# Tree-masked attention: SyncE load of fp32 queries, warmed TensorE, leading transposes and a split last pair

## The chip, the cores and the metric

The kernel runs on one core of one Trainium2 chip. The metric is the device time of one execution in microseconds (us). A kernel's profile is that of one execution; its span is about 1.8 us shorter than the device time of the same execution.

## The reference, cut to what matters

```python
batch, heads, seq, dim = 8, 12, 512, 64          # Q, K, V: float32 (8, 12, 512, 64)
# mask[i, j] = 1 where j is i or an ancestor of i in a binary heap, else 0
scores = einsum('bhqd,bhkd->bhqk', Q, K) / sqrt(dim) + (1 - mask) * (-1e9)
weights = softmax(scores, axis=-1)
out = einsum('bhqk,bhkd->bhqd', weights, V)      # float32
```

Each of the three inputs and the output has 12.58 MB. The work is done in 48 pairs of heads, six for each batch.

## The kernel before

Cuts are marked with `# ...`.

```python
ptile = consts.tile([P, perm_np.shape[1]], bf16)        # permutations, identity first
nc.sync.dma_start(out=ptile[:, :], in_=perm_dram.ap())
ctile = consts.tile([P, code_np.shape[1]], bf16)        # mask codes, 128 x 1152
nc.vector.memset(ctile[:, :], 0.0)
for p in (0, 64):
    nc.sync.dma_start(out=ctile[p:p + 32, :], in_=code_dram.ap())
# ...
plan = [(0, Q, 0, 0, 4), (0, K, 0, 0, 4), (0, V, 0, 0, 6),
        (0, Q, 0, 4, 8), (0, K, 0, 4, 8), (0, V, 0, 6, H),
        (0, Q, 0, 8, H), (0, K, 0, 8, H), (0, Q, 1, 0, 4), # ...
# load(): GpSimd's queue, cast from fp32 to bf16 on the way
nc.gpsimd.dma_start(out=loaded[kind, b][:, h0:h1, :],
                    in_=src[b, h0:h1].rearrange("h (p t) d -> p h (t d)", t=T))
# ...
# values(i): one PSUM tile for all pairs, scaled and written in one go
o2 = psumO.tile([P, 2, 512], fp32)                      # psumO has one buffer
# ... 32 matmuls ...
nc.vector.reciprocal(out=rec, in_=o4[:, :, :, D:D + 1])
nc.vector.tensor_tensor(out=of4, in0=o4[:, :, :, 0:D], in1=rec, op=ALU.mult)
# ...
load(0, 14); transposes(0); scores(0)                   # ...
for i in range(N):
    # ... loads and GpSimd stores ...
    if i >= 4 and i + 2 < N: transposes(i + 2)
    if i + 1 < N:            scores(i + 1)
    values(i)
    if i >= N - 2:           store(nc.sync, i, 1)
    if i < 4:                transposes(i + 2)
```

The softmax here doesn't subtract the row's maximum and nothing guards it: scores larger than these inputs give would overflow.

## Time and profile before

| | kernel before |
|---|---|
| median time before the prediction | 137.62 us (3 runs) |
| span of the profiled execution | 136.5 us |
| DMA busy from 5.5 to 131 us, weighed by packets | 0.95 to 1.05 in nearly every microsecond |
| ScalarE, TensorE busy | 79%, 80% |
| last store issued | 131.60 us |
| last DMA packet ends | 135.3 us |

The profiled execution took 138.32 us, 0.7 us more than the median of the timed ones. A second profile of the same kernel, taken later (run c_before), has a span of 136.3 us; spans of its other executions lie between 135.4 and 137.3 us. So a difference of a few tenths between two single profiles says nothing, and below it is the medians and the packet counts that carry the argument.

**How the work of the DMA engines is counted.** The packet records give the size, start and duration of each packet, but not the engine. Each packet is weighed by an estimate of the engine time that it needs when nothing hinders it, from the rates and the short packets of the traces (41.6 ns for a 512-byte load packet, 42.5 for 1024 bytes, 163 for a 4096-byte store, 95 for a 2304-byte packet of codes, 660 for 16 KB of instructions, about four times a 4096-byte packet; the shortest one in the traces took 884), and the sum is divided by sixteen. "Work by 9 us" is this sum for packets that start between 0 and 9 us, in us per engine. It measures how much of the job is done, where a busy share only says that something is in flight. The whole job is 129.7 us.

### The profile page before, as it was taken

How to read it: one execution, taken by the hardware profiler on the slowest of the kernel's cores; microseconds unless marked ns; L12 is line 12 of the kernel's file. 1: busy time of each engine (PE TensorE's matmuls, PEld its weight loads, DVE VectorE, ACT ScalarE, POOL GpSimd, SP SyncE). 2: the span in 40 equal slices, each digit the busy share in tenths (PEclk: the TensorE clock that was granted, in tenths of full speed). 3: DMA queues.
4: the chain of work that ended last, by engine and by line, in shares of the span. 5: the costliest groups of instructions: out<-in, count | busy, mean ns of one | idle time of the engine just before them, and what ended most of it. 6: DMA issues, size and time to landing. Idle time of an engine off the chain costs nothing.

```text
span 136.5 us, 5468 instructions
## 1 busy us (share of the span) xinstructions
PE 109.5 (80%) x2400; PEld 80.0 (59%) x2400; DVE 98.7 (72%) x214; ACT 108.2 (79%) x145; POOL 90.4 (66%) x119
## 2 busy tenths in 40 slices
PE   0078886999986699998998998999699979989610
PEld 0035664667664467786776776777376747757400
DVE  4019678798999997889887878879677869844420
ACT  3027878799986969998998999899599979998600
POOL 6969976985696993429854497475944799932200
PEclk9999999999999999999999999999999999999995
DMA  3999999999999999999999999999999999999991
GB/s 77 165 189 197 197 197 196 197 198 198 196 199 198 198 198 199 198 244 236 195 302 253 270 207 201 338 225 272 196 248 305 246 290 240 389 377 389 394 354 41
DMA packets 41815, 32.11 MB, mean 235 GB/s; under 512 B 1280, under 2 KB 38784, under 8 KB 41792
## 3 DMA queue, kind: packets, MB, share of 16 engines
q0 software_dynamic: 41008, 30.94, 125.4%
q1 hardware_dynamic: 784, 0.84, 2.1%
q8 instruction: 18, 0.29, 0.8%
q14 instruction: 5, 0.04, 0.1%
HBM read 38.06 MB, written 12.58 MB: 371 GB/s over the span
## 4 chain that ended last, share of the span: by engine, by line
PE 41%; DVE 27%; DMA 19%; issue 5%; POOL 4%; POOLq 0%
PE o L393 16%; DVE vx L281 12%; PE st L341 10%; DVE of L407 9%; DMA qs<-in_Q_dram 7%; PE stx L341 7%; DMA out_dram<-of 7%; PE tqs L295 5%; DMA vs<-in_V_dram 5%; DVE qt L315 4%; PE tk L295 4%; DVE rec L402 3%; POOL out_dram L414 3%; POOL qs L235 1%; POOL ks L235 1%
## 5 line engine op out<-in xcount | busy, mean ns | idle before, releaser
L354 ACT ACTIVATE et<-st 128x1024 bf16<-128x1024 f32 x48 | 49.4, 1029 | 4.0 <-PE st L341 3.6
L316 ACT COPY kt<-tk 128x512 bf16<-128x512 bf16 x48 | 28.3, 590 | 15.3 <-PE tk L295 14.9
L365 ACT ACTIVATE etx<-stx 128x768 bf16<-128x768 f32 x48 | 38.9, 810 | 0.3 <-PE stx L341 0.3
L281 DVE COPY vx<-vs 32x1536 bf16<-32x1536 bf16 (+3 forms) x60 | 36.2, 603 | 3.8 <-DMA vs<-in_V_dram 2.2
L407 DVE TENSOR_TENSOR of<-o,rec 128x512 f32<-128x512 f32 x48 | 33.2, 692 | 1.7
L281 POOL COPY v<-vs 32x768 bf16<-32x768 bf16 (+1 forms) x40 | 30.2, 756 | 2.7 <-DMA vs<-in_V_dram 1.0
L295 PE MATMUL tqs<-ptile,qs 128*64 128x128 bf16 x384 | 20.1, 224 | 11.1 <-DMA qs<-in_Q_dram 6.7
L393 PE MATMUL o<-vx,etx 128*64 128x65 bf16 (+1 forms) x576 | 26.7, 198 | 2.6 <-DVE vx L281 1.5
L341 PEld LDWEIGHTS <-kt 64*128 64x128 bf16 x480 | 20.3, 95 | 11.3 <-ACT kt L316 3.6
L414 POOL DMA_DIRECT2D out_dram<-of x23 | 18.0, 784 | 11.1 <-DVE of L407 3.2
L402 DVE RECIPROCAL rec<-o 128x8 f32<-128x8 f32 x48 | 9.9, 207 | 20.6 <-PE o L393 19.3
L235 POOL DMA_DIRECT2D qs<-in_Q_dram x21 | 16.9, 806 | 11.4 <-PE o L393 4.3
L315 DVE COPY qt<-tqs 128x512 bf16<-128x512 bf16 x48 | 20.1, 418 | 6.0 <-PE tqs L295 5.1
L295 PEld LDWEIGHTS <-qs 128*64 128x64 bf16 x384 | 15.4, 111 | 12.9 <-DMA qs<-in_Q_dram 6.7
L235 POOL DMA_DIRECT2D ks<-in_K_dram x21 | 16.6, 788 | 9.7 <-DMA ks<-in_K_dram 4.2
L393 PEld LDWEIGHTS <-etx 128*64 128x64 bf16 (+1 forms) x576 | 19.5, 105 | 5.8 <-issue 3.2
L295 PE MATMUL tk<-ptile,ks 128*64 128x128 bf16 x384 | 20.4, 223 | 2.9 <-issue 2.1
L393 PE MATMUL o<-v,et 128*128 128x65 bf16 x384 | 20.3, 194 | 1.2 <-DVE of L407 1.1
L341 PE MATMUL st<-qt,kt 64*128 64x512 bf16 x96 | 18.7, 385 | 2.3 <-DVE qt L315 2.1
L341 PE MATMUL st<-ctile 64*128 64x512 bf16 x96 | 19.2, 396 | 0.1
L341 PEld LDWEIGHTS <-ctile 64*128 64x128 bf16 x192 | 11.0, 94 | 13.1 <-issue 3.0
L341 PE MATMUL stx<-qt,kt 64*128 64x128 bf16 (+1 forms) x384 | 17.9, 211 | 0.2 <-issue 0.2
(13 smaller groups left out, 58.2 us busy)
## 6 DMA issues: line engine op xcount, KB each, us to landing
out_dram<-of POOLq DMA_DIRECT2D x23, 512.0 KB, 10.7
vs<-in_V_dram POOLq DMA_DIRECT2D x6, 768.0 KB, 15.4
qs<-in_Q_dram POOLq DMA_DIRECT2D x9, 384.0 KB, 15.4
ks<-in_K_dram POOLq DMA_DIRECT2D x9, 384.0 KB, 15.3
qs<-in_Q_dram POOLq DMA_DIRECT2D x9, 256.0 KB, 11.1
ks<-in_K_dram POOLq DMA_DIRECT2D x9, 256.0 KB, 11.7
vs<-in_V_dram POOLq DMA_DIRECT2D x4, 384.0 KB, 10.1
out_dram<-of SPq DMA_DIRECT2D x2, 256.0 KB, 5.0
```

The source lines that it names most:

```text
L235: nc.gpsimd.dma_start(out=loaded[kind, b][:, h0:h1, :], in_=src[b, h0:h1].rearrange("h (p t) d -> p h (t d)", t=T),)
L281: (eng or nc.vector.tensor_copy)(out=o, in_=i)
L295: nc.tensor.matmul(out=o[D * hi:D * hi + D], rhs=perms[mat], lhsT=src[:, 2 * hp + hi, D * t:D * t + D], start=True, stop=True, is_transpos ...
L315: nc.vector.tensor_copy(out=qt[:, :], in_=tq)
L316: nc.scalar.copy(out=kt[:, :].rearrange("d (i j x) -> d i j x", j=2, x=32), in_=tk[:, :].rearrange("d (j i x) -> d i j x", j=2, x=32)[:, 0:8],
L341: nc.tensor.matmul(out=dst, lhsT=lhsT, rhs=rhs, start=first, stop=True, skip_group_check=not first,)
L354: nc.scalar.activation(out=et1[:, :, :], in_=st1[:, :, :], func=AF.Exp, scale=scale)
L365: nc.scalar.activation(out=etx[:, :, :, 32:P], in_=stx[:, :, :].rearrange("p h (t q) -> p h t q", t=T)[:, :, :, 32:P], func=AF.Exp, scale= ...
L393: nc.tensor.matmul(out=o2[p0:p1, hi, (D + 1) * t:(D + 1) * (t + 1)], lhsT=e[:, hi, P * t + p0:P * t + p1], rhs=v, start=hi not in (m[0] fo ...
L402: nc.vector.reciprocal(out=rec[:, :, :, :], in_=o4[:, :, :, D:D + 1])
L407: nc.vector.tensor_tensor(out=of4, in0=o4[:, :, :, 0:D], in1=rec[:, :, :, :].to_broadcast([P, 2, T, D]), op=ALU.mult,)
L414: eng.dma_start(out=out[b, 2 * hp:2 * hp + 2 * n].rearrange("h (p t) d -> p h (t d)", t=T), in_=done[i // 2][:, 2 * (i % 2):2 * (i % 2) + ...
```

## The change

Its intent: four heads of Q come as fp32 by SyncE's queue, which can start before GpSimd's, and are cast by GpSimd in SBUF; nine identity matmuls bring TensorE to full clock while it waits; transposes go ahead of the scores from pair 1 on, not from pair 4; the last pair's values go to a scores bank that is free, and each of its heads is scaled and stored by itself.

```diff
+    first = consts.tile([P, 4, T * D], fp32)
+    nc.sync.dma_start(
+        out=first[:, :, :], in_=Q[0, 8:12].rearrange("h (p t) d -> p h (t d)", t=T)
+    )
     ptile = consts.tile([P, perm_np.shape[1]], bf16)
@@
-            (0, Q, 0, 8, H), (0, K, 0, 8, H), (0, Q, 1, 0, 4), (0, K, 1, 0, 4),
+            (0, K, 0, 8, H), (0, Q, 1, 0, 4), (0, K, 1, 0, 4),
@@ values(i); last = i == N - 1
+        if last:
+            o2 = psumS.tile([P, 2, 512], fp32, name="st1")
+        else:
+            o2 = psumO.tile([P, 2, 512], fp32)
@@ ... scaled per head where last, and then
+            if last:
+                store((nc.sync, nc.scalar)[h0], i, h0, h1)
@@ at the start
+        for n in range(9):
+            nc.tensor.matmul(out=warm[:, n % 2, :], lhsT=perms[0],
+                             rhs=ptile[:, 0:512], start=True, stop=True)
-        load(0, 14)
+        load(0, 10)
+        nc.gpsimd.tensor_copy(out=loaded["q", 0][:, 8:12, :], in_=first[:, :, :])
+        load(0, 13)
@@ in the loop
-            if i >= 4 and i + 2 < N:
+            if i == 0:
+                scores(1)
+            if i + 2 < N:
                 transposes(i + 2)
-            if i + 1 < N:
+            if 0 < i < N - 1:
                 scores(i + 1)
             values(i)
-            if i < 4:
-                transposes(i + 2)
```

More of the change, by code (lines that the diff above doesn't have):

```diff
@@ L180 @@
     AHEAD = 12
-    FIRST = (16, 18, 20, 22, 24)
+    FIRST = (15, 17, 19, 21, 23)
     LATE = 10
@@ L379, in values @@
         )
-        o2 = psumO.tile([P, 2, 512], fp32)
+        last = i == N - 1
+        if last:
+            o2 = psumS.tile([P, 2, 512], fp32, name="st1")
+        else:
+            o2 = psumO.tile([P, 2, 512], fp32)
         full, part = [], []
@@ L391, in values @@
         mms = full + part
+        if last:
+            mms.sort(key=lambda m: m[0])
         for n, (hi, p0, p1, t, e, v) in enumerate(mms):
@@ L399, in values @@
             )
-        o4 = o2[:, :, 0:T * (D + 1)].rearrange("p h (t x) -> p h t x", t=T)
-        rec = work.tile([P, 2, T, 1], fp32)
-        nc.vector.reciprocal(out=rec[:, :, :, :], in_=o4[:, :, :, D:D + 1])
         if i % 2 == 0:
@@ L405, in values, with store @@
         of = done[i // 2][:, 2 * (i % 2):2 * (i % 2) + 2, :]
+        o4 = o2[:, :, 0:T * (D + 1)].rearrange("p h (t x) -> p h t x", t=T)
         of4 = of.rearrange("p h (t d) -> p h t d", t=T)
-        nc.vector.tensor_tensor(
-            out=of4, in0=o4[:, :, :, 0:D],
-            in1=rec[:, :, :, :].to_broadcast([P, 2, T, D]), op=ALU.mult,
-        )
-    def store(eng, i, n):
+        rec = work.tile([P, 2, T, 1], fp32)
+        for h0, h1 in ((0, 1), (1, 2)) if last else ((0, 2),):
+            nc.vector.reciprocal(
+                out=rec[:, h0:h1, :, :], in_=o4[:, h0:h1, :, D:D + 1]
+            )
+            nc.vector.tensor_tensor(
+                out=of4[:, h0:h1, :, :], in0=o4[:, h0:h1, :, 0:D],
+                in1=rec[:, h0:h1, :, :].to_broadcast([P, h1 - h0, T, D]),
+                op=ALU.mult,
+            )
+            if last:
+                store((nc.sync, nc.scalar)[h0], i, h0, h1)
+    def store(eng, i, h0, h1):
         b, hp = pairs[i]
         eng.dma_start(
-            out=out[b, 2 * hp:2 * hp + 2 * n].rearrange(
+            out=out[b, 2 * hp + h0:2 * hp + h1].rearrange(
                 "h (p t) d -> p h (t d)", t=T
             ),
-            in_=done[i // 2][:, 2 * (i % 2):2 * (i % 2) + 2 * n, :],
+            in_=done[i // 2][:, 2 * (i % 2) + h0:2 * (i % 2) + h1, :],
         )
@@ L434 @@
                 deal[i] = (b + 1, 0, H, hp, hp + 1)
-        load(0, 14)
+        warm = psumO.tile([P, 2, 512], fp32, name="o2")
+        for n in range(9):
+            nc.tensor.matmul(
+                out=warm[:, n % 2, :], lhsT=perms[0], rhs=ptile[:, 0:512],
+                start=True, stop=True,
+            )
+        load(0, 10)
+        nc.gpsimd.tensor_copy(out=loaded["q", 0][:, 8:12, :], in_=first[:, :, :])
+        load(0, 13)
         transposes(0)
@@ L446 @@
             while 2 * len(stored) + 1 <= min(upto, N - 3):
-                store(nc.gpsimd, 2 * len(stored), 2)
-            if i >= 4 and i + 2 < N:
+                store(nc.gpsimd, 2 * len(stored), 0, 4)
+            if i == 0:
+                scores(1)
+            if i + 2 < N:
                 transposes(i + 2)
-            if i + 1 < N:
+            if 0 < i < N - 1:
                 scores(i + 1)
             values(i)
-            if i >= N - 2:
-                store(nc.sync, i, 1)
-            if i < 4:
-                transposes(i + 2)
+            if i == N - 2:
+                store(nc.sync, i, 0, 2)
             if i in deal:
```

## The prediction

> **What bounds the kernel now.** I read four views, in this order: the page's slices and queue table, the windows in half and whole microseconds, the groups by line with the timeline of the start, and the timeline and chain of the last ten microseconds.
>
> The page comes first because it names the candidate. The slices of the DMA row are full from the second to the last but one, while no compute engine is above 80%:
>
> ```profile
> PE 109.5 (80%) x2400; PEld 80.0 (59%) x2400; DVE 98.7 (72%) x214; ACT 108.2 (79%) x145; POOL 90.4 (66%) x119
> ...
> DMA  3999999999999999999999999999999999999991
> ...
> q0 software_dynamic: 41008, 30.94, 125.4%
> q1 hardware_dynamic: 784, 0.84, 2.1%
> q8 instruction: 18, 0.29, 0.8%
> ...
> HBM read 38.06 MB, written 12.58 MB: 371 GB/s over the span
> ```
>
> The GB/s row counts what is written: a load reads fp32 and writes bf16, so 197 GB/s in a pure load stage is 394 GB/s read from HBM, and a pure store stage shows 385 to 395. Both kinds thus pass at one rate of about 0.39 MB per us. The inputs are 37.75 MB and the output 12.58 MB, together 50.33 MB, which is 128 us at 394 GB/s. That leaves 8.5 of the 136.5 us in which the DMA engines do not run at this rate, and nearly all of them lie at the two ends:
>
> ```profile
> 1.00:1.50 0.50, 0.00 (x0) 0.00 (x0) 0.50 (x2) 0.50 (x1) 0.23 (x1) 1.00 0.00 0
> 1.50:2.00 0.50, 0.00 (x0) 0.00 (x0) 0.50 (x6) 0.50 (x1) 0.50 (x1) 1.00 0.46 102
> 2.00:2.50 0.50, 0.00 (x0) 0.00 (x0) 0.31 (x5) 0.02 (x1) 0.50 (x2) 1.00 0.66 223
> 2.50:3.00 0.50, 0.00 (x0) 0.00 (x0) 0.00 (x0) 0.00 (x0) 0.50 (x2) 1.00 0.52 129
> 3.00:3.50 0.50, 0.00 (x0) 0.00 (x0) 0.00 (x0) 0.00 (x0) 0.50 (x1) 1.00 0.80 84
> 3.50:4.00 0.50, 0.00 (x0) 0.00 (x0) 0.00 (x0) 0.00 (x0) 0.50 (x2) 1.00 0.85 91
> 4.00:4.50 0.50, 0.00 (x0) 0.00 (x0) 0.00 (x0) 0.00 (x0) 0.50 (x2) 1.00 1.10 161
> 5.50:6.00 0.50, 0.00 (x0) 0.00 (x0) 0.00 (x0) 0.00 (x0) 0.50 (x1) 1.00 1.47 198
> 132.00:133.00 1.00, 0.00 (x0) 0.00 (x0) 0.00 (x0) 0.00 (x0) 0.00 (x0) 0.78 0.83 299
> 133.00:134.00 1.00, 0.00 (x0) 0.00 (x0) 0.00 (x0) 0.00 (x0) 0.00 (x0) 0.50 0.39 140
> 134.00:135.00 1.00, 0.00 (x0) 0.00 (x0) 0.00 (x0) 0.00 (x0) 0.00 (x0) 0.50 0.13 45
> ```
>
> The last two columns are the DMA share and GB/s. At the start, constants trickle in from 1.5 us and the loads reach full rate at 5.5 us. At the end the rate falls to 45 GB/s after 134: that is not an idle DMA but two of the sixteen engines still working. In the trace's packet records fourteen engines are done at 133.3 us, one at 134.6 and one at 135.25, and the last two run without a pause (4096-byte packets at 164 ns alternating with 1024-byte ones at 42 ns, then the latter alone). So the slowest DMA engine, never dry from about 5 us to 135.25, sets the end, and 1.3 us of completion follow.
>
> I also weighed every packet by its unhindered time (41.6 ns a 512-byte load packet, 164 ns a 4096-byte store packet, 660 ns a 16 KB instruction packet) and divided by sixteen engines: from 5.5 to 131 us the share used is 0.95 to 1.05 in nearly every microsecond (0.83 and 0.85 at 113 to 115). Compute is a second, nearly as long path:
>
> ```profile
> 128.28 0.69 DVE L407 TENSOR_TENSOR of<-o,rec 128x512 f32<-128x512 f32 x1
> 129.00 3.00 SPq L414 DMA_DIRECT2D out_dram<-of  x2
> ...
> 129.12 0.40 PE L393 MATMUL o<-v,et 128*128 128x65 bf16 x8 [1.12 <-DVE of L407]
> ...
> 130.88 0.69 DVE L407 TENSOR_TENSOR of<-o,rec 128x512 f32<-128x512 f32 x1
> ```
>
> The last pair's values wait 1.12 us until VectorE has emptied the one values bank of the pair before, so the last store is issued at 131.57. Only a few tenths of slack separate the two paths, so cutting one alone is not enough; the change cuts both.
>
> **What the Trainium skill says.** "DMA: Bandwidth & Descriptors", section "Issuing engines are not separate DMA queues": DMAs from ScalarE, SyncE or GpSimd run on the same sixteen engines and interleave. So SyncE's queue brings no bandwidth, only an earlier start; the trace agrees, since the SyncE stores at the end share the engines with GpSimd's. The same page, section "SWDGE vs HWDGE vs iDMA": a cast during a DMA is for GpSimd's queue alone, which is why this block comes as fp32 and is cast by an instruction. "TensorE: Matmul & The Clock Gate", Part 1: TensorE starts at half clock, N/1.2 ns a matmul, and goes to full clock after some 3.4 us of activity. The trace agrees in kind: two scores matmuls side by side take 0.61 us at 8.70 and 0.38 at 34.51, and the fast times begin near 12.9 us; the page's clock row, a different quantity, stays at full. "Runtime: NRT & Kernel Launch", section "Instruction fetch mechanics": instructions come in 16 KiB blocks by DMA; the trace has 18 such packets with 0.29 MB in all.
>
> **Part 1, four heads of Q in fp32 by SyncE.** It removes 512 KB of fp32 reading, 524,288 bytes at 394 GB/s = 1.33 us, from GpSimd's stream, and one GpSimd issue of 0.80 us. It adds the same 524,288 bytes to SyncE's queue, issued at 0.74 us, ahead of the constants; 512 packets of 1024 bytes at 42.5 ns over 16 engines are 1.36 us of engine time. The gain is how much of that fits in time that is idle now. By weighed packets the idle shares of the half microseconds from 1.5 to 5.5 are 0.72, 0.39, 0.65, 0.65, 0.66, 0.34, 0.10 and 0.17, in sum 3.68 halves = 1.84 us. SyncE's first bytes move at 1.7 us now, and its queue is ahead of GpSimd's, whose first packet moves at 2.95; so some 1.6 us are open to it for 1.36 us of work. Ramp and descriptor making will not pack it perfectly: I take 1.2 us, 0.7 to 1.4.
>
> Its price falls on compute. SyncE has 836 KB instead of 312 to move early, so the first Q, K and V blocks, landing at 6.75, 8.1 and 10.07 us now, come about 1 us later, and the constants too. GpSimd casts 128x1024 fp32, once: its 32x768 bf16 copies take 0.82 to 0.97 us, 1.1 to 1.3 ns an element along a row, so 1.2 us, perhaps 2 with fp32 input. It stands before further load issues, but 10 loads (6.03 MB, 15.3 us) are by then queued from 2.95 on, so until after 19 us; GpSimd should issue again near 16. The stream does not run dry.
>
> **Part 2, nine identity matmuls.** 128x512 at half clock is 0.43 us each, 3.8 us at most, started when the constants land near 4 us, thus done by about 7.8, when the first Q lands. They cost at most some tenths and give the first pair full clock: pair 0's transposes, scores and values lose some 0.2 us in each of about five groups, 1 us, which pays for the later landing.
>
> **Part 3, transposes lead from pair 1.** In the chain, values of pairs 0 to 4 begin at 13.61, 16.44, 19.28, 22.11 and 25.76 us: 2.83 us a pair and once 3.65, through output scaling, Q copy, scores, values. Later pairs take 2.06 to 2.24 (33.00 to 35.24; 52.09 to 54.15), near ScalarE's 108.2/48 = 2.25. So 4 x 0.6 = 2.4 us of compute time. It is off the DMA path and makes slack there.
>
> **Part 4, the last pair.** The values go to a scores bank already read, which removes the 1.12 us wait; the first head is scaled and stored while the second is made. ScalarE's last exponent ends at 128.46, its 12 full and partial matmuls follow in under 0.6 us, and four short VectorE instructions of 0.2 to 0.4 us. The last store is issued near 130.1, 1.4 us earlier than now, at unchanged times before it.
>
> **Sum.** Compute ends 1.4 + 2.4 - 0.5 or so earlier, by some 3 us unless it catches up with the loads. DMA ends 1.2 us earlier. The later path counts: the slowest engine goes from 135.25 to 134.05, with the same 1.3 us behind it: span 135.3, from 136.5. Off the median 137.62, that is 136.4 us, 0.9% less.
>
> **Rivals.** (a) Compute is the real bound and the DMA only full because work is queued ahead: then 3 us come off, 134.6 us, faster by over 2%. For it: the DMA chain joins VectorE's line at 128.29, 0.04 us after that was ready anyway. Against: the engines are at 1.0 from 5.5 us to 131, and bytes do not shrink. (b) The early transfer is no gain: SyncE's block merely pushes GpSimd's first loads back, or the cast delays issues and the stream runs dry near 19 us, which costs what it gave: 137.4 to 138 us. For it: the DMA share is already 0.5 to 0.8 at 2 to 4 us. Against: weighed by packets that time is two thirds idle. (c) The tail of the two late engines is not bytes but luck of instruction fetches (one 16 KB packet begins at 128.1 us); it can move by one packet, 0.7 to 1.0 us either way, with the changed length of TensorE's program: 135.6 or 137.2.
>
> **Range and chances.** The start gain of 0.7 to 1.4 and the tail's play of about half a us give 136.4 with 135.5 to 137.2. Faster by over 2% needs 134.87, that is rival (a) or a perfect start with a shorter tail: 0.08. Slower needs 140.4: 0.01. Within 2%: 0.91.
>
> **What would show it.** Right: in the changed profile the GB/s of 1.5 to 4 us rise to 250 to 350, loads run at 197 from about 5 us on without a dip at 17 to 20; values of pairs 1 to 4 come 2.2 to 2.4 us apart; the last store is issued by 130.5, and yet the last bytes move near 134, some 4 us later. Wrong: the end follows the last store by the present 4.9 us at an earlier time (then compute was the bound), or the DMA row has a new gap.

## The result, and the profile after

The changed kernel took **138.04 us** (137.91 to 138.13, 4 runs), the kernel before 137.69 us in the same rounds (137.56 to 137.77). The ratio is 1.0026, with a 95% interval of 1.0008 to 1.0043. A second series (run after_again) gave 1.0018 (0.9996 to 1.0040). So the change made the kernel some 0.2 to 0.3% slower or left it as it was; the 1.2 us that I had predicted to come off did not.

From the page of the changed kernel: its span, the DMA row and the GB/s in forty slices, and SyncE's queue.

```profile
span 136.3 us, 5491 instructions
...
DMA  4999999999999999999999999999999999999981
GB/s 111 229 181 196 197 197 196 198 197 198 196 199 200 196 201 196 198 243 235 197 308 249 269 212 208 327 238 257 199 253 302 241 298 245 394 386 394 387 334 37
...
q1 hardware_dynamic: 1184, 1.23, 2.9%
```

The middle is what it was. The second slice shows more, 229 GB/s, but a block that lands as fp32 counts twice what a cast load counts for the same bytes read. The third shows 181, where the kernel before has 189 and a pure load stage 197.

The windows of half a microsecond, for comparison with those that the prediction shows; the last two columns are DMA share and GB/s:

```profile
1.50:2.00 0.50, 0.00 (x0) 0.00 (x0) 0.50 (x6) 0.50 (x1) 0.50 (x1) 1.00 0.57 18
2.00:2.50 0.50, 0.00 (x0) 0.00 (x0) 0.31 (x5) 0.02 (x1) 0.50 (x2) 1.00 0.30 63
2.50:3.00 0.50, 0.00 (x0) 0.00 (x0) 0.00 (x0) 0.00 (x0) 0.50 (x2) 1.00 1.04 360
...
3.50:4.00 0.50, 0.00 (x0) 0.00 (x0) 0.00 (x0) 0.00 (x0) 0.50 (x2) 1.00 1.09 388
...
7.50:8.00 0.50, 0.50 (x3) 0.17 (x2) 0.00 (x0) 0.00 (x0) 0.04 (x1) 1.00 1.24 137
...
8.50:9.00 0.50, 0.50 (x5) 0.21 (x6) 0.00 (x0) 0.00 (x0) 0.39 (x1) 1.00 1.43 195
```

The gap of 2.5 to 4 us is indeed filled: 360 and 388 GB/s of SyncE's block where there were 129 and 91. But the loads now reach their full rate at 8.5 us. In the kernel before they first reach it at 5.5, dip to 175 and 167 GB/s from 6.5 to 7.5, and hold it from there. Counted by packets, the changed kernel is ahead by 0.64 us at 4 us (1.60 against 0.96), and at 9 us by 0.28 (5.81 against 5.53). In its second profile and in the second profile of the kernel before it is behind: 5.51 against 5.63. GpSimd's first load packet starts at 4.14 us where it started at 2.95.

The timeline of the start of the changed kernel (start, duration, engine, line, operation, and in brackets the idle time before and what ended it):

```profile
4.83 4.02 PE L455 MATMUL o<-ptile 128*128 128x512 bf16 x9 [4.83 <-DMA ptile<-tree_perms]
...
8.79 0.64 PE L300 MATMUL tqs<-ptile,qs 128*64 128x128 bf16 x8
...
11.68 2.09 DVE L286 COPY vx<-vs 64x768 bf16<-64x768 bf16 x4 [1.79 <-DMA vs<-in_V_dram]
```

The first transposes begin at 8.79 us, 2.0 us later than the 6.75 before, and the first V copies at 11.68 and not at 10.07. The transposes of Q still take 0.64 us, as before; those of K that follow take 0.41 where they took 0.64, so TensorE is warm from there on. In the second profile of the same kernel (after_again) it is not, after the same nine matmuls:

```profile
9.93 0.64 PE L300 MATMUL tk<-ptile,ks 128*64 128x128 bf16 x8 [0.66 <-DMA ks<-in_K_dram]
```

The end of the changed kernel, in the timeline:

```profile
127.75 0.20 PE L404 MATMUL st<-vx,etx 128*128 128x65 bf16 x1 [0.30 <-ACT etx L370]
...
129.22 0.47 PE L404 MATMUL st<-vx,etx 128*128 128x65 bf16 x5 [1.27 <-issue]
...
131.19 0.42 DVE L421 TENSOR_TENSOR of<-st,rec 128x256 f32<-128x256 f32 x1
131.65 0.37 ACTq L432 DMA_DIRECT2D out_dram<-of  x1
```

The values no longer wait for VectorE. In this execution TensorE pauses for 1.27 us in the middle of the last pair for nothing that the profile shows, so the last store goes out at 131.65 us, as late as before. Below it will be seen that this does not matter.

### The profile page after: what moved, and what is told of

The parts are those of the page before. It is cut to its first block, busy times and chain, and to the rows that moved or that the text cites. A ratio compares the mean times of both kernels' runs of the same rounds, so it can differ in the third digit from the quotient of the medians.

```text
span 136.3 us, 5491 instructions
## 1 busy us (share of the span) xinstructions
PE 112.6 (83%) x2409; PEld 81.1 (59%) x2409; DVE 100.2 (74%) x216; ACT 107.9 (79%) x145; POOL 90.7 (67%) x119
## 4 chain that ended last, share of the span: by engine, by line
DMA 62%; POOL 11%; PE 11%; issue 6%; ACT 3%; DVE 2%; POOLq 0%; ACTq 0%
DMA ks<-in_K_dram 41%; DMA vs<-in_V_dram 20%; POOL v L286 5%; PE o L404 3%; POOL qs L240 2%; PE st L346 2%; ACT etx L370 2%; POOL ks L240 2%; PE stx L346 2%; PE tk L300 1%; PE tqs L300 1%; POOL vs L240 1%; DVE of L421 1%; PE st L404 1%; ACT et L359 1%
## 5 line engine op out<-in xcount | busy, mean ns | idle before, releaser
L286 DVE COPY vx<-vs 32x1536 bf16<-32x1536 bf16 (+3 forms) x60 | 37.5, 625 | 3.3 <-DMA vs<-in_V_dram 1.8
L421 DVE TENSOR_TENSOR of<-o,rec 128x512 f32<-128x512 f32 x47 | 32.5, 691 | 1.6
L286 POOL COPY v<-vs 32x768 bf16<-32x768 bf16 (+1 forms) x40 | 29.7, 742 | 2.6 <-DMA vs<-in_V_dram 0.9
L240 POOL DMA_DIRECT2D qs<-in_Q_dram x20 | 16.2, 812 | 10.7 <-PE o L404 4.5
L240 POOL DMA_DIRECT2D ks<-in_K_dram x21 | 17.1, 814 | 8.4 <-DMA ks<-in_K_dram 3.1
L404 PE MATMUL o<-v,et 128*128 128x65 bf16 x376 | 19.8, 194 | 0.0
L346 PE MATMUL stx<-qt,kt 64*128 64x96 bf16 (+1 forms) x384 | 17.7, 209 | 0.4 <-issue 0.4
```

Source lines behind the costliest of these rows:

```text
L240: nc.gpsimd.dma_start(out=loaded[kind, b][:, h0:h1, :], in_=src[b, h0:h1].rearrange("h (p t) d -> p h (t d)", t=T),)
L286: (eng or nc.vector.tensor_copy)(out=o, in_=i)
L346: nc.tensor.matmul(out=dst, lhsT=lhsT, rhs=rhs, start=first, stop=True, skip_group_check=not first,)
L404: nc.tensor.matmul(out=o2[p0:p1, hi, (D + 1) * t:(D + 1) * (t + 1)], lhsT=e[:, hi, P * t + p0:P * t + p1], rhs=v, start=hi not in (m[0] fo ...
L421: nc.vector.tensor_tensor(out=of4[:, h0:h1, :, :], in0=o4[:, h0:h1, :, 0:D], in1=rec[:, h0:h1, :, :].to_broadcast([P, h1 - h0, T, D]), op= ...
```

## The experiments

Two theories stood after the result. **Theory A**: the DMA engines bound the kernel, and SyncE's block only pushes back what came after it. **Theory B**: the end is set by compute and by that pause of TensorE, whatever the DMA engines do. Each run had 6 timed executions, against 11 or 12 of the kernel before on the same chip.

| run | median us | before, same rounds | ratio (95% interval) | GpSimd's first packet, us | work by 9 us | whole job |
|---|---|---|---|---|---|---|
| c_before | 137.86 | 138.03 | 0.9987 (0.9962 to 1.0012) | 2.93 | 5.63 | 129.7 |
| p1_only | 138.17 | 138.03 | 1.0017 (0.9979 to 1.0055) | 4.01 | 5.66 | 129.7 |
| no_p1 | 137.91 | 138.03 | 0.9992 (0.9963 to 1.0022) | 2.86 | 5.60 | 129.7 |
| no_p2 | 137.82 | 138.03 | 0.9983 (0.9958 to 1.0008) | 4.14 | 5.52 | 129.7 |
| after_again | 138.16 | 137.84 | 1.0018 (0.9996 to 1.0040) | 4.12 | 5.51 | 129.8 |
| no_bytes (wrong) | 136.64 | 137.84 | 0.9927 (0.9901 to 0.9954) | 2.85 | 5.53 | 128.4 |
| first_late | 137.88 | 137.84 | 1.0003 (0.9983 to 1.0024) | 2.98 | 5.58 | 129.8 |
| first_half | 137.94 | 137.84 | 1.0007 (0.9981 to 1.0033) | 3.17 | 5.54 | 129.8 |
| before_no_codes (wrong) | 137.88 | 137.84 | 1.0006 (0.9979 to 1.0033) | 2.86 | 5.15 | 129.3 |
| after_no_codes (wrong) | 137.17 | 137.84 | 0.9948 (0.9930 to 0.9966) | 4.04 | 5.89 | 129.4 |
| before_wide | 137.85 | 137.84 | 0.9998 (0.9973 to 1.0022) | 3.26 | 5.75 | 130.1 |
| after_wide | 138.58 | 137.84 | 1.0051 (1.0022 to 1.0080) | 4.08 | 5.34 | 130.2 |
| p1_no_codes (wrong) | 137.41 | 138.04 | 0.9954 (0.9913 to 0.9996) | 3.86 | 5.83 | 129.3 |
| after_codes_first | 137.70 | 138.04 | 0.9970 (0.9936 to 1.0004) | 3.23 | 6.07 | 129.8 |
| before_codes_first | 138.00 | 138.04 | 0.9988 (0.9950 to 1.0026) | 3.17 | 5.82 | 129.7 |
| after_codes_once | 137.01 | 138.04 | 0.9925 (0.9891 to 0.9958) | 3.50 | 6.03 | 129.6 |
| before_codes_once | 138.16 | 137.79 | 1.0019 (0.9992 to 1.0046) | 2.92 | 5.16 | 129.5 |
| codes_once_again | 137.17 | 137.79 | 0.9962 (0.9924 to 1.0001) | 3.92 | 5.68 | 129.6 |

"Wrong" marks kernels whose results are wrong, since data were left out. The packet columns are from one profile each.

### Which part does what

**c_before**: the kernel before, unchanged.

> The kernel before, unchanged, as a control: time ratio 1.000 within 0.001. It also gives a second profile of the kernel before: its first profile came from an execution of 138.32 us, 0.7 us above the median of its timed runs. If that profile was an untypical one, this profile's span is near 135.9 us and not 136.5; which interval is shorter (the start up to 9 us, the middle, or the end after 131 us) shows where executions of one kernel differ.

The ratio was 0.9987: 0.0013 from 1 where 0.001 was expected, and well inside the interval. The second profile of the same kernel has work by 9 us of 5.63 where the first has 5.53, and no pause of TensorE in its last pair: both vary by execution.

**p1_only**: the kernel before with part 1 alone.

```diff
+    first = consts.tile([P, 4, T * D], fp32)
+    nc.sync.dma_start(out=first[:, :, :], in_=Q[0, 8:12].rearrange(...))
-            (0, Q, 0, 8, H), (0, K, 0, 8, H), ...
+            (0, K, 0, 8, H), ...
-        load(0, 14)
+        load(0, 10); nc.gpsimd.tensor_copy(out=loaded["q", 0][:, 8:12, :], in_=first); load(0, 13)
```

> The kernel before with part 1 alone (four heads of Q in fp32 by SyncE, cast by GpSimd). Theory A (the early block only pushes GpSimd's stream back: its first packet from 2.95 to about 4.1 us, first Q landing near 8.7 instead of 6.75): 0 to +0.5 us, 137.6 to 138.2 us. Theory B (the end is set by TensorE's instruction fetch in the last pair, whatever the start does): no change beyond 0.1 us. My prediction on record: -1.2 us.

138.17 us: no gain, and my 1.2 us lie far outside the interval. The block is worth 0.78 us at 4 us (1.74 against 0.96) and 0.03 to 0.13 at 9 us. GpSimd's stream starts at 4.01 us. That is within what theory A expected, and the interval does not exclude theory B's "no change" either.

One rival has to be named here. As in the kernel before, parts 2 to 4 are missing. In this profile the last store is issued only at 132.08 us, and the DMA engines do not stay full until it comes (the line of its window from 132 to 133 us):

```profile
132.00:133.00 1.00, 0.00 (x0) 0.00 (x0) 0.05 (x1) 0.00 (x0) 0.00 (x0) 1.00 0.52 188
```

In the next microsecond the rate is 276 GB/s again. So in this execution late compute may have cost a few tenths; before_no_codes, below, shows the same (last store at 132.52 us; 184 GB/s, then 231).

**no_p1**: the changed kernel without part 1.

```diff
-    first = consts.tile([P, 4, T * D], fp32)   # and its load, its cast, its place in the plan
+            (0, Q, 0, 8, H), ...               # as in the kernel before
```

> The changed kernel without part 1 (warming, leading transposes and the split last pair stay). Theory A: 137.2 to 137.6 us, faster than the kernel before by 0.1 to 0.5 us and than the changed kernel by 0.5 us or more, first values before 13.5 us. Theory B: the same as the changed kernel, near 138.0, with a pause of about 1.2 us of TensorE marked issue in the last pair.

137.91 us, equal to the kernel before and within noise of the others: above the 137.2 to 137.6 us of theory A and near the 138.0 of theory B, but the interval decides neither. The pause of 1.2 us that theory B expected is one of 0.45. The timeline of its last pair decides more:

```profile
127.73 0.37 PE L400 MATMUL st<-vx,etx 128*128 128x65 bf16 x5 [0.45 <-issue]
...
129.84 0.37 ACTq L428 DMA_DIRECT2D out_dram<-of  x1
```

Its last store is issued at 129.84 us, 1.3 to 1.8 us earlier than in the two profiles of the kernel before (131.18 and 131.60), and nothing comes off: its last DMA packet ends at 134.8, theirs at 135.0 and 135.3. In after_again the last store goes out at 129.34, 2.3 us earlier than in the first profile of the same kernel, and the last packet 0.4 us earlier. Theory B, as a rule for whatever store time, falls with this.

**no_p2**: the changed kernel without the nine identity matmuls.

```diff
-        warm = psumO.tile([P, 2, 512], fp32, name="o2")
-        for n in range(9):
-            nc.tensor.matmul(out=warm[:, n % 2, :], lhsT=perms[0], rhs=ptile[:, 0:512], ...)
```

> The changed kernel without the nine identity matmuls. If they hold up the start (they run from 4.8 to 8.85 us, as the first Q lands, and the DMA engines stand at 0.7 to 0.9 of their rate just then) it is 0.2 to 0.6 us faster than the changed kernel, 137.4 to 137.8, and the share of DMA from 5 to 8.5 us rises to 1.0. If they are harmless: 137.9 to 138.2, DMA share there unchanged. TensorE's program is 18 instructions shorter, so its fetches fall elsewhere in the last pair.

The ratio, 0.9983, is below those of the changed kernel (1.0026 and 1.0018), but they were taken in other series, and the intervals touch. The loads ramp up as slowly as with the matmuls (work by 9 us 5.52), so nothing shows that TensorE's reading slows the DMA engines. Whether warming costs 0.3 us in another way is left open.

### Do the DMA engines set the end?

**after_again**: the changed kernel, unchanged, on the chip of the next three.

> The changed kernel once more, on the same chip as the three below: within 0.4 us of the kernel before (its first figures were 138.04 against 137.69). Its profile again: first packet of GpSimd's stream near 4.1 us; work done by 9 us, weighed by packets, 5.5 to 5.8 us an engine, against 5.5 to 5.6 in the kernel before.

**no_bytes**: the same without SyncE's load.

```diff
-    nc.sync.dma_start(out=first[:, :, :], in_=Q[0, 8:12].rearrange(...))
+    nc.vector.memset(first[:, :, :], 0.0)
```

> The changed kernel with SyncE's load of four heads of Q taken out (the tile is filled with zeros by VectorE; four heads of the output are wrong on purpose). The DMA engines have 512 KB less to do, 1.33 us. If the DMA engines bound the kernel from the start to the last byte: 1.1 to 1.6 us faster than the changed kernel, the first packet of GpSimd's stream back near 2.9 us, work by 9 us again 5.4 to 5.7. If compute or TensorE's instruction fetch sets the end: within 0.3 us of the changed kernel.

It took 136.64 us: 0.9927/1.0018 = 0.991 of the changed kernel, 1.25 us less, for 1.36 us of transfers taken out of the DMA engines (128.4 against 129.8 us of work). The cast, the matmuls and the stores are all still there. Compute also starts earlier in it, but that is not what made it shorter: its last store is issued at 129.70 us, in after_again at 129.34, and yet after_again's last packet ends 1.4 us later. Two windows of the end, first of the changed kernel, then of this one:

```profile
131.00:133.00 2.00, 0.00 (x0) 0.00 (x0) 0.58 (x3) 0.00 (x0) 0.00 (x0) 0.50 0.76 278
133.00:136.50 3.50, 0.00 (x0) 0.00 (x0) 0.00 (x0) 0.00 (x0) 0.00 (x0) 0.50 0.09 32
```

```profile
131.00:133.00 2.00, 0.00 (x0) 0.00 (x0) 0.00 (x0) 0.00 (x0) 0.00 (x0) 0.50 0.40 142
133.00:136.50 3.50, 0.00 (x0) 0.00 (x0) 0.00 (x0) 0.00 (x0) 0.00 (x0) 0.50 0.01 2
```

The engines have run dry earlier: the last packet ends at 133.2 us, in the two profiles of the changed kernel at 134.6 and 135.0. So the kernel ends when the bytes are through, more exactly when the last engines are: before the end there is a stretch with fewer than six packets in flight, 0.6 to 2.3 us long in the profiles (1.9 and 2.1 in the two of the kernel before, 1.9 and 0.8 in the two of the changed kernel; the records name no engine, so the prediction's "fourteen engines are done" is itself read from packets in flight). The prediction's rival (c), that this tail is luck, was not tested; a tail that varies by 1.7 us is as large as the effects looked for here. This part of the prediction holds, and the question is only why the head start was not one.

**first_late**: SyncE's block behind the constants, held back until 2.35 us.

```diff
+    nc.vector.memset(first[:, 0, 0:8], 0.0)      # after the other fills; the load then waits for it
+    nc.sync.dma_start(out=first[:, :, :], in_=Q[0, 8:12].rearrange(...))   # moved here
```

> The changed kernel with SyncE's load of four heads of Q issued behind the constants (it waits for a small VectorE fill at 2.3 us). If the early burst does harm by standing in front of GpSimd's first packets: the first packet of GpSimd's stream comes near 3 us again, the gap of 3 to 4.5 us is filled, work by 9 us rises to 6.2 to 6.6 us, and the time falls by 0.6 to 1.1 us against the kernel before. If GpSimd's queue needs its slow start of about 2 us whatever else runs, and other traffic only stretches it: work by 9 us 5.5 to 5.8, time within 0.3 us of the changed kernel.

**first_half**: two heads of Q in place of four, in front.

```diff
-    first = consts.tile([P, 4, T * D], fp32)     # Q[0, 8:12]
+    first = consts.tile([P, 2, T * D], fp32)     # Q[0, 8:10]; (0, Q, 0, 10, H) stays in the plan
```

> The changed kernel with two heads of Q in place of four by SyncE (256 KB in front of the constants; the other two as in the kernel before). If the burst harms only by what reaches past 2.9 us, where GpSimd's stream could begin: first packet of that stream at 3.2 to 3.5 us, work by 9 us 5.9 to 6.2, 0.2 to 0.6 us faster than the kernel before. If any early burst is paid back in full: first packet near 3.5, work by 9 us within 0.2 of 5.6, time within 0.3 us.

Both came out equal to the kernel before, with work by 9 us of 5.58 and 5.54, that is, each as in the second of its two expected outcomes. In first_late the block is issued at 2.35 us, but its packets move from 5.2 to 8.0, since they stand in the same queue behind the packets of the mask codes, which move from 2.5 to 4.5 us. The gap of 3 to 4.5 us stays as it was. In first_half the block is over at 3.1 us, and the codes spread to 6.7. The form of this last result led on to a guess: wherever the codes lay, there the loads were slow.

### The mask codes

The codes are 147 KB in two loads of 32 partitions each, 64 packets of 2304 bytes. Unhindered they are 0.4 us of work per engine. In the kernel before they move from 2.6 to 4.6 us, that is, in the gap; in the changed kernel from 4.5 to 7.2, on top of GpSimd's loads. In both kernels single packets of them take up to 1.2 us.

**before_no_codes** and **after_no_codes**: the kernel before and the changed one without the load.

```diff
     nc.vector.memset(ctile[:, :], 0.0)
-    for p in (0, 64):
-        nc.sync.dma_start(out=ctile[p:p + 32, :], in_=code_dram.ap())
```

> The kernel before without the load of the mask codes (147 KB in 64 packets of 2304 bytes; the tile stays zero, results wrong on purpose). So far the work done by 9 us has been 5.5 to 5.8 us an engine in every kernel, and the slow stretches have followed the code packets wherever they lay (2.5 to 5 us in the kernel before, 4.5 to 7 in the changed one and without the Q bytes), single ones of them taking up to 1.2 us. If these packets hold up the engines: the GpSimd stream is at full rate from 3.5 us, work by 9 us 6.2 to 6.9 although 0.38 less is asked for, time 0.8 to 1.5 us shorter than before. If the slow stretch is the GpSimd queue's own start: work by 9 us 5.0 to 5.4, time 0.3 to 0.5 us shorter (the bytes alone).

> The changed kernel without the load of the mask codes (wrong on purpose). If the code packets are what gives SyncE's head start back: work by 9 us 6.8 to 7.4, 0.5 us or more above the kernel before without codes, and 0.5 to 1.2 us faster than it; 2 us faster than the kernel before. If the burst is paid back in any case: work by 9 us and time within 0.3 us of the kernel before without codes.

Taking the codes out of the kernel before gains nothing (1.0006): the 0.4 us that are no longer asked for are missing from its work by 9 us (5.15), so **the codes had cost nothing that could be measured where they lay**. (This profile has the late last store named under p1_only, so compute may hide a few tenths.) Of the two outcomes expected, the work fits the second (5.0 to 5.4), the time neither. Taking them out of the changed kernel gains about 1.0 us (0.9948 against 1.0018 and 1.0026). And without codes the changed kernel beats the one before it: 0.9948/1.0006 = 0.994, or 0.8 us, with work by 9 us ahead by 0.74. The gain over it is as expected; work by 9 us (5.89, not 6.8 to 7.4) and "2 us faster than the kernel before" are not.

**p1_no_codes**: the kernel before with part 1 alone, without the codes.

```diff
     # p1_only, and
-    for p in (0, 64):
-        nc.sync.dma_start(out=ctile[p:p + 32, :], in_=code_dram.ap())
```

> The kernel before with part 1 alone and without the load of the mask codes (wrong on purpose). If the block gains only where no codes come behind it: 0.4 to 0.9 us faster than the kernel before without codes (which was equal to the kernel before), so 137.0 to 137.5 where the kernel before has 137.84; work by 9 us 5.6 to 6.0 against 5.15. If parts 2 to 4 made the difference: within 0.3 us of the kernel before.

137.41 us, 0.9954 with a wide interval, or 0.7 us against before_no_codes: by that, nearly all of the 0.8 us is part 1's. Its worth is there when the codes do not come behind it.

**before_wide** and **after_wide**: the codes in one load over 128 partitions, with zeros between, and no fill to wait for.

```diff
-    nc.vector.memset(ctile[:, :], 0.0)
-    for p in (0, 64):
-        nc.sync.dma_start(out=ctile[p:p + 32, :], in_=code_dram.ap())
+    nc.sync.dma_start(out=ctile[:, :], in_=code_dram.ap())      # 128 rows in DRAM
```

> The kernel before with the codes loaded by one transfer over all 128 partitions (295 KB with zeros between, right results, no VectorE fill to wait for). If it is the shape over 32 partitions that stalls the engines: code packets of near 100 ns, full rate from 3.5 us, work by 9 us 6.3 to 6.9, of which 0.38 is the added zeros; time 0.4 to 1.0 us shorter than before. If any code load at that moment stalls them: work by 9 us near 5.6 and a time 0.2 to 0.5 us longer.

> The changed kernel with the codes in one transfer over 128 partitions (right results). If the shape of the code load is the cause: work by 9 us 6.6 to 7.2, time 0.5 to 1.5 us shorter than the changed kernel, the best of all with right results. If not: within 0.4 us of the changed kernel, or slower by the added 0.4 us.

The shape is not the cause: before_wide is equal to the kernel before (0.4 us more work, in the gap), and after_wide, at 138.58, the slowest of all, has packets of codes of up to 1.27 us and the lowest work by 9 us of the changed kernels.

**after_codes_first** and **before_codes_first**: codes, permutations, then the block (in the first of them); the fill takes other rows, so that no load waits for it.

```diff
+    for p in (0, 64):
+        nc.sync.dma_start(out=ctile[p:p + 32, :], in_=code_dram.ap())
+        nc.vector.memset(ctile[p + 32:p + 64, :], 0.0)
     nc.sync.dma_start(out=ptile[:, :], in_=perm_dram.ap())
+    nc.sync.dma_start(out=first[:, :, :], in_=Q[0, 8:12].rearrange(...))   # not in before_codes_first
```

> The changed kernel with SyncE's queue in the order codes, permutations, block of Q; the zero fill takes only rows that no load writes, so the codes are issued at 0.74 us (right results). If codes behind the block give its gain back: work by 9 us 6.0 to 6.4, 0.4 to 0.9 us faster than the kernel before. If GpSimd's stream pays for any burst in front of it: work by 9 us 5.4 to 5.8, within 0.3 us of the kernel before.

> The kernel before with the codes in front of the permutations and no wait for the fill: control for the run above, no block of Q. Codes over by 3 us, GpSimd's stream free of them from its first packet. If the codes cost nothing in the gap: time within 0.3 us of the kernel before, work by 9 us 5.3 to 5.7.

137.70 and 138.00 us in the same rounds: work by 9 us rises to 6.07, as expected of order as the cause, but the gain of 0.3% has an interval that includes none. The block is now late itself; its packets move from 4.8 to 7.2 us.

**after_codes_once** and **before_codes_once**: the codes loaded once, in front, and copied to the other half by VectorE, with and without the block. **codes_once_again** repeats the first.

```diff
+    nc.sync.dma_start(out=ctile[0:32, :], in_=code_dram.ap())
+    for p in (32, 96):
+        nc.vector.memset(ctile[p:p + 32, :], 0.0)
     nc.sync.dma_start(out=ptile[:, :], in_=perm_dram.ap())
+    nc.sync.dma_start(out=first[:, :, :], in_=Q[0, 8:12].rearrange(...))   # not in before_codes_once
@@
         transposes(0)
+        nc.vector.tensor_copy(out=ctile[64:96, :], in_=ctile[0:32, :])
```

> The changed kernel with the codes loaded once (72 KB, first in SyncE's queue) and copied to the other half by VectorE, which is idle then (right results). 0.2 us less DMA work than with both loads. If codes behind the block are the cause: 0.5 to 1.0 us faster than the kernel before, the best right one. If any burst is paid back: at most 0.3 us faster.

> The kernel before with the codes loaded once, first in SyncE's queue, and copied by VectorE; no block of Q (right results). If the block is what gains: within 0.35 us of the kernel before (the codes were free in the gap), work by 9 us 5.4 to 5.7. If the codes' load is what cost: 0.7 us or more faster than the kernel before.

> The kernel after_codes_once unchanged, a second time: ratio to the kernel before 0.990 to 0.996; work by 9 us 5.9 to 6.2.

after_codes_once is the best kernel with right results: 137.01 us and 0.9925 on one chip, 137.17 and 0.9962 on another, that is, 1.0 and 0.5 us faster than the kernel before (the second interval just reaches 1; its profile, with work by 9 us of 5.68, is of its slowest execution, 138.37 us). Without the change the same loads of codes give 1.0019, so the gain is not theirs but that of the four parts: on that chip 0.9962/1.0019 = 0.994, 0.8 us. That it is the block's is what p1_no_codes says. In the second round two expectations were missed, work by 9 us of 5.16 (5.4 to 5.7) and of 5.68 (5.9 to 6.2). SyncE's issues, first in the changed kernel, then in after_codes_once:

```profile
0.74 0.43 SPq L169 DMA_DIRECT2D first<-in_Q_dram  x1
...
1.23 0.49 SPq L173 DMA_DIRECT2D ptile<-tree_perms  x1
...
1.77 0.88 SPq L177 DMA_DIRECT2D ctile<-tree_codes  x2
```

```profile
0.74 0.34 SPq L169 DMA_DIRECT2D ctile<-tree_codes  x1
1.14 0.41 SPq L173 DMA_DIRECT2D ptile<-tree_perms  x1
1.60 0.49 SPq L175 DMA_DIRECT2D first<-in_Q_dram  x1
```

The same three things in the other order, and one load of codes less. The codes are over at 2.1 us; the block moves from 2.9 to 6.7 us among GpSimd's first packets, which begin at 3.50 and not at 4.14.

## Why the prediction was wrong, point by point

The prediction gave 136.4 us, 135.5 to 137.2; measured were 138.04 in its rounds. The class, within 2%, was right, and the direction was not.

- **"What bounds the kernel now": right.** 512 KB less made the kernel 1.25 us shorter, for an expected 1.33, and last stores issued 1.3 to 2.3 us earlier made it at most 0.4 us shorter. "Only a few tenths of slack" was too little for those runs, where the last store could move from 129.3 to 131.65 us for 0.4 us at the end; from about 132 us on the engines do run short (p1_only, before_no_codes). The kernels' times follow, roughly, what is left to do at 9 us (whole job less work by 9 us): 122.9 us in no_bytes, 123.5 to 123.6 in after_no_codes, p1_no_codes and after_codes_once, 123.7 to 124.3 in the two kernels compared and all others of nearly unchanged time, 124.8 in after_wide. In the profiled executions themselves the span exceeds that rest by 11.5 to 12.9 us, so a single profile says little.
- **Part 1: the step that failed.** It read: "The gain is how much of that fits in time that is idle now ... so some 1.6 us are open to it for 1.36 us of work ... I take 1.2 us". The block did go into the gap, from 1.8 to 3.9 us, but what it displaced was not subtracted: the codes and permutations, 0.8 us of work that had lain there, the codes at no measurable cost (before_no_codes: 1.0006), and the start of GpSimd's stream. The codes' packets went to 4.5 to 7.2 us, on top of GpSimd's loads; with them there the changed kernel is about 1.0 us slower than without them (after_no_codes), more than their own 0.4. GpSimd's stream began 1.2 us later and lost 0.8 and 1.2 us from its first packet to 9 us, much as before (1.1 in both profiles).

  Of GpSimd's own loads (its 512-byte packets alone), 4.7 and 4.8 us of work were done by 9 us in the two profiles of the kernel before, 3.6 and 3.3 in those of the changed one, 4.0 to 4.1 in after_no_codes and p1_no_codes: of a block of 1.36 us, 1.1 to 1.5 are paid back with the codes behind it and 0.6 to 0.7 without. The codes on the stream do not do it by themselves: in no_bytes they lie there as well (4.5 to 7.1 us), without the block, and those loads stand at 4.7 by 9 us, as in the kernel before. (By its time, 1.0 us below the kernel before for 1.3 us less work, some 0.3 us of cost remain possible.)

  In work by 9 us the gain was 0.28 us in one profile and negative in the other. Rival (b), "SyncE's block merely pushes GpSimd's first loads back", was the right one, and its 137.4 to 138 us nearly held the result; the words against it, that the time "is two thirds idle", measured the gap and not what would be moved out of it.
- **The price on compute: right in kind, too small.** The first Q, K and V came 1.6 to 2.0 us later, not 1 (1.9 to 2.8 later than in c_before, where the first Q is used at 5.95). The cast took 1.03 us, within what was said; GpSimd issued its next load at 15.19, and the stream never ran dry.
- **Part 2: not reliable, and late.** The nine matmuls took 4.02 us, 0.45 each, and ended at 8.85 and not 7.8, since their constants stood behind the block. "Give the first pair full clock" was luck: of the 11 profiles with these matmuls, pair 0's transposes of K take 0.41 us in 7 and still 0.64 in 4 (after_again, first_late, first_half, after_no_codes). The 3.4 us of activity that the prediction counted on were not enough in those four.
- **Part 3: the size was right.** Values of pairs 0 to 4 begin at 15.5, 18.2, 20.3, 23.3 and 25.4 us: 2.5 us a pair against 3.0 by the prediction's own list, which makes up the 2 us of late start by pair 4 and no more.
- **Part 4: shown for the mechanism, without use.** The wait of 1.12 us is gone. A pause of TensorE of 1.27 us took its place in the profiled execution; other profiles with part 4, with last stores at 129.3 to 129.8 (after_again, no_p1, no_p2, no_bytes), had it shorter or elsewhere. By after against after_again, the end depended on it by 0.4 us at most.
- **Sum.** 1.2 us was to come from the start and came out as none. Why the changed kernel is 0.2 to 0.3% slower and not equal is not settled: p1_only leans the same way (1.0017) but its interval includes 1.

**What stays open.** In most kernels the engines work at 0.3 to 0.95 of their rate between GpSimd's first packet and about 8 or 9 us, in some without any codes (before_no_codes: 0.5 to 0.8 from 5 to 8 us), and lose 0.8 to 1.5 us by it; the least, 0.4 us, is lost in after_codes_first and after_codes_once. I have shown that the changed kernel is slower with the codes behind its block than without them; no_bytes says that codes on GpSimd's stream alone do not do it. How block and codes act together, and what the rest is, no run here separates. That the order alone suffices is not shown either: after_codes_first gains 0.3% with an interval that includes none. Nor is it shown why packets of codes take up to 1.2 us, or why GpSimd's first packet came only near the end of the block in the kernels in which the block was first.

## What to carry to other kernels

A gap at the start of a kernel bound by its transfers is only worth what is left of it after everything that already moves in it, or was about to start in it, has found a new place: list what stands in the same queue behind the new transfer and where it will land. Try small loads that others wait for in front of a large one that nobody waits for yet; here the version that did so with half the codes was the best one with right results. And count done work (bytes or weighed packets by a fixed time), not busy shares: here the DMA share of 2.5 to 4 us rose to full while the work done by 9 us hardly changed.

## What the Trainium skill lacked or had wrong

- "DMA: Bandwidth & Descriptors", "Specifications", gives a first-byte latency of about 1 us for GpSimd's queue and about 0.6 for SyncE's. Here SyncE's first packet moved 0.97 us after the start of its issue (0.74 to 1.71 us), and GpSimd's 1.7 us after (1.26 to 2.95), in the kernel before. Counted from the end of the issues (1.09 and 2.15 us) it is 0.62 and 0.80, which fits; the section does not say from where it counts.
- The same page, "Issuing engines are not separate DMA queues", says that transfers of several engines interleave. It lacks what a burst does to the start of another queue: with 512 KB in front, SyncE's packets ran alone at full rate from 2.5 to 4 us, and GpSimd's first packet came at 3.9 to 4.1 us in six kernels and not at 2.9, although its load had been issued by 2.15 us.
- No page has the slow start of a load stream: from the first packet to 9 us it cost 0.4 to 1.5 us of work per engine in the kernels here, 1.1 in the kernel before.
- "Runtime: NRT & Kernel Launch", "Instruction fetch mechanics", agrees on the 16 KiB blocks (18 packets of 16,384 bytes) but calls crossing them mostly hidden. Here such a packet takes 0.88 to 1.2 us among other traffic, and TensorE has pauses of up to 1.3 us marked issue in its stream, one of which ends 1.5 us after such a packet landed at 127.7 us; that the fetch causes them fits, but is not shown.
